# Weight halves of three projections added by transfers instead of VectorE, and four heads scaled during earlier scans

## The chip, the cores and the metric

The kernel runs on one core of one Trainium2 chip. The metric is the device time of one execution in microseconds (us), as the median of several runs. A profile of one execution shows what every engine did: TensorE (PE, its weight loads PEld), VectorE (DVE), ScalarE (ACT), GpSimd (POOL), and SyncE (SP), which here only issues transfers.

## The reference

Two requests, of 512 and 256 tokens, go through the same two layers of an encoder, 1024 wide. Each layer is `x += 1/2 FFN; x += mixer; x += 1/2 FFN` with an RMS norm ahead of each part. The mixer of the first layer is a gated linear recurrence run in both directions, with 8 heads of 128; that of the second layer is windowed attention. The change concerns the recurrent mixer alone:

```python
q, i, g, f_fw, f_bw = jnp.split(x @ w_in, 5, axis=-1)
...
o_fwd = gla_chunk_scan(q, k_f, i, logf_f)
o_bwd = rev(gla_chunk_scan(rev(q), rev(k_b), rev(i), rev(logf_b)))
o = (o_fwd + o_bwd).astype(F32)
o = o * lax.rsqrt(jnp.mean(o * o, axis=-1, keepdims=True) + NORM_EPS)
o = o * g_norm.astype(F32).reshape(H, V)
o = o.reshape(B, T, H * V).astype(x.dtype) * jax.nn.silu(g)
return o @ w_o
```

So the output of every head is divided by its own root mean square, gated with silu(g), and projected.

## The kernel before

All 768 tokens are treated together, as 6 blocks of 128 tokens or two halves of 384. Every operand of a large matrix product is split into a high part (a cast on ScalarE) and a low part (a subtraction on VectorE), and a product is made of three matmuls, high x high, high x low and low x high (`split`, `mm3`).

Large products are done by a fast scheme with seven products of half-sized blocks, p1 to p7, in place of eight. The weight matrix is cut into four blocks a11, a12, a21, a22, and the scheme needs sums of them. In the mixer three projections work so: **v** (the reference's `i`), **g** and the output projection **o**. `tok_steps` prepares their weights. It fetches the four blocks with transfers on SP's queue (each block as one tile `wr` of 128x1024 for the first half of its depth, kp = 0, and two tiles `tA` of 128x512 for the second, kp = 1), fetches a21 a second time into `s3`, and adds, with accumulating transfers on GpSimd's queue (`into`, line 147), a11 to that copy and a22 to a21. What it returns are 14 steps, one for each product and kp, in the order of the products: `TOK` for v and g (p1, p2, p7, p6, p5, p4, p3), `OUT` for o (p1, p2, p3, p7, p6, p4, p5). A step splits the block that its product needs into two tiles `w` (lines 323 and 324). There are 8 such tiles, so steps run as earlier products give theirs back.

Two more sums are needed. The "second" is a11 + a21, for p6; the "fourth" is a12 plus that, for p3. Before, both are additions on VectorE: in v and g ahead of the split of p6 and of p3 (line 260), in o both behind the split of p2 (line 272). They are held in program order. Every other instruction is ordered within its engine by a planner, which takes the program's order as a priority and has a model of durations; each engine's queue then runs strictly in the order that was planned.

`tok_quad` runs the seven products on TensorE (line 764). Several products share an accumulation bank: in o, p7 goes on in the bank of p3 after ScalarE has copied p3 out (line 1140). After p1 and p2 of o, `mixed` makes the sums of the activation blocks on VectorE (`mix`, lines 426 to 432) and splits them; line 1147 adds p2 to the residual.

Between v and g lie the eight scans, one for each head. A scan has seven levels: ScalarE copies the keys into a packed order (line 857), TensorE forms scores (line 827), VectorE merges them through masks (line 846) and multiplies queries (line 879), keys (line 883) and decays (line 885). After the levels come transposes, states and outputs (lines 900 to 938), and the sum of squares of the head's output goes into `hss` (line 939). `weave` puts pieces of other TensorE work between the levels: products for the gates and queries of the following heads (`stream`; lines 318 to 320, with sigmoids at line 803), and, from the end of the seventh scan on, the projection g (`gate`).

The norm of the heads is `rstds` (a square root on ScalarE, line 1030, which needs a table load, and a reciprocal, line 1031) and `scaled` (for each head six multiplications of 128x128 on ScalarE, line 1078). Before, the heads 0 to 6 get their `rstds` after the seventh scan, and each is scaled behind one level of the eighth scan; head 7 follows after it.

Of the kernel before, what the change touches and what calls it, by code (L numbers as in the profile page):

```python
# [25 lines left out]
HEADS = 8  # L26
# [18 lines left out]
TOK = ("p1", "p2", "p7", "p6", "p5", "p4", "p3")  # L45
TCHAIN = {"p2": "p1", "p4": "p5", "p3": "p7"}
OUT = ("p1", "p2", "p3", "p7", "p6", "p4", "p5")
# [5 lines left out]
class Trunk:  # L53
# [174 lines left out]
    def tok_steps(self, key, srcs, order):  # L228
        nc = self.nc
        flat = lambda t: t.rearrange("p a b -> p (a b)")  # L230

        def fetch(src):
            t = self.wp.tile([P, 1024], F32, tag="wr", name=self.name("wr"), bufs=RAWBUFS)
            nc.sync.dma_start(t.rearrange("p (a b) -> p a b", a=2), src[0])
            parts = [[t], [self.tmp(512), self.tmp(512)]]
            for a, t in enumerate(parts[1]):
                self.last_load = nc.sync.dma_start(t, src[1][:, a, :])
            return parts

        a11, a12, a21, a22 = (fetch(src) for src in srcs)  # L240
        more = self.big([P, 2, 512])
        s3 = [
            [self.wp.tile([P, 512], F32, tag="s3", name=self.name("s3"), bufs=2) for _ in range(2)],
            [more[:, a, :] for a in range(2)],
        ]
        for kp in range(2):
            for a, t in enumerate(s3[kp]):
                self.last_load = nc.sync.dma_start(t, srcs[2][kp][:, a, :])
                self.into(t, a11[0][0][:, a * 512 : (a + 1) * 512] if kp == 0 else a11[1][a])
            for t, u in zip(a21[kp], a22[kp]):  # L250
                self.into(t, u)
        own = {"p1": a11, "p2": a12, "p3": a12, "p4": a22, "p5": a21, "p6": a11, "p7": s3}
        second, fourth = (a11, a21), (a12, a11)
        sums = {"p6": (second,), "p3": (fourth,)} if order == TOK else {}
        behind = {"p2": (second, fourth)} if order == OUT else {}

        def step(name, kp):
            for total, part in sums.get(name, ()):
                for t, u in zip(total[kp], part[kp]):
                    self.tc.keep_in_program_order(nc.vector.tensor_add(t, t, u))  # L260
            hi, lo = self.wtile(), self.wtile()
            at = 0
            for src in own[name][kp]:
                n = src.shape[-1]
                h, l = (t[:, at : at + n] for t in (hi, lo))
                self.split(src, h, l)
                at += n
            view = lambda t: t.rearrange("p (a b) -> p a b", a=2)
            self.staged[(*key, name, kp)] = (view(hi), view(lo), 2)
            for total, part in behind.get(name, ()):  # L270
                for t, u in zip(total[kp], part[kp]):
                    self.tc.keep_in_program_order(nc.vector.tensor_add(t, t, u))

        return [(2, lambda name=name, kp=kp: step(name, kp)) for name in order for kp in range(2)]

    def stage_next(self):
# [698 lines left out]
    def hgrn(self, lb_row, gn_row, next_row):  # L975
        nc = self.nc
# [4 lines left out]
        heads = [{} for _ in range(HEADS)]  # L981
# [35 lines left out]
        scan = lambda hd: self.hgrn_scan(hd, vs)  # L1017

        def stream():
            for h in range(1, HEADS):  # L1020
                for c in (0, 3, 4):
                    if (h, c) not in LEAD:
                        yield from self.hgrn_chunk(h, heads[h], c, range(2))
                self.hgrn_gates(h, heads[h])
# [3 lines left out]
        def rstds(a, b):  # L1028
            r = rs[:, a:b, :]
            nc.scalar.activation(r, self.hss[:, a:b, :], AF.Sqrt, bias=self.eps, scale=1.0 / P)  # L1030
            nc.vector.reciprocal(r, r)
# [42 lines left out]
        def scaled(first, last):  # L1074
            for b in range(NBLK):
                for h in range(first, last):
                    u = vs[b][:, h * P : (h + 1) * P]
                    nc.scalar.activation(u, u, AF.Copy, scale=rs[:, h, b : b + 1])
# [21 lines left out]
        def gate():  # L1100
            need = {"p1": "t3", "p2": "t2", "p7": "t1", "p6": "t4"}
            for at in self.tok_quad(("g",), TOK, TCHAIN, self.ops, evac_g):
                if at[1:] == (HB - 1, 1) and at[0] in need:
                    self.reload_factor(need[at[0]])
                yield at

        feed = itertools.chain(stream(), gate())
        for h in range(HEADS - 1):
            self.weave(scan(heads[h]), feed, 16 if h == 0 else 18)
        rstds(0, HEADS - 1)  # L1110
        self.weave(scan(heads[-1]), feed, 20, also=lambda i: i < HEADS - 1 and scaled(i, i + 1))
        rstds(HEADS - 1, HEADS)
        scaled(HEADS - 1, HEADS)
        for i in range(HB):
# [441 lines left out]
```

## Time and profile before

| | |
|---|---|
| median of 3 runs | 2783.34 us (2783.18 to 2783.43) |
| the profiled execution: its own time | 2783.55 us |
| its span in the trace | 2781.6 us |
| TensorE busy in the span | 99% |
| mean granted TensorE clock | 0.998 |
| recurrent mixer | from about 503 to 1071 us of the span |
| v, scans, g, o on TensorE | from 542, 600, 878 and 967 us |

How to read it: a row of a timeline has start and length in us, the engine, the line of the kernel, the operation, what it writes and reads, shapes and the number of instructions merged into the row; square brackets hold the idle time of the engine before it and what ended that. "A <-B L5" means that A waited for what engine B did at line 5. Matmuls overlap, so TensorE can be busy all the time only as far as the rows show it.

### The profile page before, as it was taken

The numbers are of one execution on the slowest core, as the hardware profiler recorded it, in microseconds if no ns is written. First come the engines' busy times: TensorE is split into PE (matmuls) and PEld (weight loads), VectorE is DVE, ScalarE is ACT, GpSimd is POOL, SyncE is SP. The second block draws the span as 40 slices with busy tenths as digits, with TensorE's granted clock in tenths as the row PEclk, the third lists the DMA queues.
The fourth block names the chain that finished last, engine by engine and source line by source line (L and its number), as shares of the span: only waits on it lengthen the run. The fifth ranks groups of instructions, "written<-read, shape, count | busy, mean of one in ns | idle before, by whom it ended". The sixth has DMA issues, their size and how long they took to land.

```text
span 2781.6 us, 40766 instructions
## 1 busy us (share of the span) xinstructions
PE 2750.1 (99%) x15117; PEld 2555.3 (92%) x15117; DVE 2228.3 (80%) x3825; ACT 1387.6 (50%) x2586; POOL 393.9 (14%) x431
## 2 busy tenths in 40 slices
PE   8999999999999999999999999999999999999998
PEld 8999999989999879999999999999888889999998
DVE  8788788777887888788878887887848878788877
ACT  7344443634445765444445543444458855444443
POOL 2111121100000001211111121111102211211111
PEclk9999999999999999999999999999999999999999
DMA  6554554731121533655444355544422123655443
GB/s 173 128 126 117 126 141 123 244 107 39 39 67 50 173 92 81 147 133 129 117 113 119 81 144 134 124 122 114 129 73 76 45 63 75 146 133 129 117 115 107
DMA packets 337351, 313.41 MB, mean 113 GB/s; under 512 B 12584, under 2 KB 258816, under 8 KB 337152
## 3 DMA queue, kind: packets, MB, share of 16 engines
q1 hardware_dynamic: 296992, 221.81, 27.1%
q0 software_dynamic: 35856, 75.51, 15.0%
q10 hardware_dynamic: 4304, 13.49, 1.3%
q8 instruction: 119, 1.95, 0.3%
q14 instruction: 80, 0.66, 0.1%
HBM read 225.82 MB, written 15.73 MB: 87 GB/s over the span
## 4 chain that ended last, share of the span: by engine, by line
PE 95%; DVE 2%; ACT 2%; DMA 0%; issue 0%; DVEq 0%; ACTq 0%
PE ps L517 42%; PE ps L581 21%; PE ps L319 6%; PE ps L318 6%; PE ps L320 6%; PE ps L764 5%; PE ps L827 3%; PE ps L932 1%; PE ps L1418 1%; PE ps L908 1%; PE ps L389 1%; PE ps L1430 0%; PE ps L1380 0%; PE ps L1381 0%; PE ps L1431 0%; PE ps L1181 0%
## 5 line engine op out<-in xcount | busy, mean ns | idle before, releaser
L517 PE MATMUL ps<-big,w 128*128 128x384 f32 x6720 | 1169.3, 334 | 0.0
L517 PEld LDWEIGHTS ps<-big,w 128*128 128x128 f32 x6720 | 1165.9, 188 | 1.7 <-ACT tA L534 0.2
L208 ACT CAST w<-wr 128x512 fp32r<-128x512 f32 x600 | 416.0, 707 | 682.6 <-PE ps L517 274.2
L581 PE MATMUL ps<-w,big 128*128 128x512 f32 x2520 | 575.6, 389 | 0.0
L581 PEld LDWEIGHTS ps<-w,big 128*128 128x128 f32 x2520 | 472.6, 188 | 97.9 <-DVE x L603 0.3
L209 DVE TENSOR_TENSOR w<-wr,w 128x512 fp32r<-128x512 f32 (+1 forms) x520 | 430.3, 831 | 156.6 <-ACT w L208 140.1
L603 DVE SCALAR_TENSOR_TENSOR x<-ps,x 128x512 f32<-128x512 f32 x468 | 301.9, 683 | 10.1 <-PE ps L320 10.0
L147 POOL DMA_DIRECT2D s<-wr x126 | 110.9, 885 | 1353.5 <-DMA s<-in_ffn_w_dram 410.0
L318 PE MATMUL ps<-big,w 128*128 128x384 f32 x640 | 219.3, 345 | 2.0 <-ACT w L175 1.0
L319 PE MATMUL ps<-big,w 128*128 128x384 f32 x640 | 215.5, 337 | 0.9 <-DVE big L324 0.9
L320 PE MATMUL ps<-big,w 128*128 128x384 f32 x640 | 214.5, 335 | 0.0
L323 ACT CAST big<-tA 128x384 fp32r<-128x384 f32 x296 | 148.0, 513 | 114.3 <-DVE tA L549 36.4
L764 PE MATMUL ps<-w,big 128*128 128x512 f32 x756 | 179.7, 395 | 3.2 <-ACT big L1140 2.6
L764 PEld LDWEIGHTS ps<-w,big 128*128 128x128 f32 x756 | 141.4, 189 | 33.5 <-ACT big L1140 3.5
L324 DVE TENSOR_TENSOR big<-tA,big 128x384 fp32r<-128x384 f32 x296 | 166.2, 572 | 6.6 <-ACT big L323 4.5
L209 POOL TENSOR_TENSOR w<-wr,w 128x512 fp32r<-128x512 f32 x80 | 136.0, 1700 | 187.2 <-ACT w L208 182.8
L147 POOL DMA_DIRECT2D wr<-wr x103 | 90.8, 882 | 459.5 <-DMA wr<-in_ffn_w_dram 175.3
L318 PE MATMUL ps<-w,big 128*128 128x512 f32 x336 | 134.7, 401 | 0.3 <-DVE big L1441 0.2
L215 DVE TENSOR_TENSOR wr<-wr,wr 128x512 f32<-128x512 f32 (+1 forms) x120 | 122.9, 1024 | 14.2 <-issue 10.2
L320 PE MATMUL ps<-w,big 128*128 128x512 f32 x336 | 132.2, 393 | 0.5 <-DVE big L404 0.5
L319 PE MATMUL ps<-w,big 128*128 128x512 f32 x336 | 131.6, 392 | 0.0
L318 PEld LDWEIGHTS ps<-big,w 128*128 128x128 f32 x640 | 119.9, 188 | 3.2 <-ACT w L175 1.3
(219 smaller groups left out, 3471.2 us busy)
## 6 DMA issues: line engine op xcount, KB each, us to landing
wr<-in_ffn_w_dram SPq DMA_DIRECT2D x264, 512.0 KB, 4.0
s<-wr POOLq DMA_DIRECT2D x126, 256.0 KB, 4.9
s<-in_ffn_w_dram SPq DMA_DIRECT2D x120, 256.0 KB, 3.3
wr<-wr POOLq DMA_DIRECT2D x80, 256.0 KB, 3.8
wr<-in_hg_w_in_dram SPq DMA_DIRECT2D x32, 512.0 KB, 3.9
wr<-wr POOLq DMA_DIRECT2D x23, 512.0 KB, 4.6
spill<-x ACTq DMA_DIRECT2D x12, 512.0 KB, 3.9
kept<-big POOLq DMA_DIRECT2D x8, 768.0 KB, 5.4
```

Source lines behind the costliest of these rows:

```text
L147: self.nc.gpsimd.dma_start(out, src, accum_op=ALU.add)
L208: nc.scalar.copy(h, src)
L209: (eng or nc.vector).tensor_sub(l, src, h.bitcast(F32))
L318: nc.tensor.matmul(out, a[0], b[0], start=first, stop=False)
L319: nc.tensor.matmul(out, a[0], b[1], start=False, stop=False)
L320: nc.tensor.matmul(out, a[1], b[0], start=False, stop=last)
L323: self.nc.scalar.copy(hi, src)
L324: self.nc.vector.tensor_sub(lo, src, hi.bitcast(F32))
L517: self.nc.tensor.matmul(ps, a[x], b[y], start=first and k == 0 and i == 0, stop=k == 3 and i == 2, skip_group_check=True,)
L581: nc.tensor.matmul(ps, a[x], w[y], start=name == chain and kp == 0 and q == 0, stop=kp == 1 and q == 2, skip_group_check=True,)
L603: self.nc.vector.scalar_tensor_tensor(x, ps, c, x, ALU.mult, ALU.add)
L764: nc.tensor.matmul(ps, x[:, sl], y, start=fresh and k == 0 and q == 0, stop=k == 3 and q == 2, skip_group_check=True,)
```

## The change

In v and g the second and the fourth sum become accumulating transfers on GpSimd's queue: a21 is added to a11 once p1's part of a11 is split, and a11 to a12 once p2's part of a12 is split. In o the second sum becomes such a transfer behind the split of p1, and the fourth stays an addition on VectorE behind the split of p2. For o the blocks are fetched in the order a21, a22, a11, a12.

The heads 0 to 3 get their `rstds` right after the fourth scan. From the fifth scan on, one of them is scaled behind the second and one behind the fifth level of a scan, as long as any are left: two in the fifth scan and two in the sixth. Heads 4 to 6 get their `rstds` after the seventh scan as before and are scaled behind the second, fourth and sixth level of the eighth.

```diff
-        a11, a12, a21, a22 = (fetch(src) for src in srcs)
+        got = {i: fetch(srcs[i]) for i in ((0, 1, 2, 3) if order == TOK else (2, 3, 0, 1))}
+        a11, a12, a21, a22 = (got[i] for i in range(4))
...
-        second, fourth = (a11, a21), (a12, a11)
-        sums = {"p6": (second,), "p3": (fourth,)} if order == TOK else {}
-        behind = {"p2": (second, fourth)} if order == OUT else {}
+        behind = {"p1": (a11, a21), "p2": (a12, a11)}
+        add = self.into if order == TOK else lambda t, u: self.tc.keep_in_program_order(nc.vector.tensor_add(t, t, u))
 
         def step(name, kp):
-            for total, part in sums.get(name, ()):
-                for t, u in zip(total[kp], part[kp]):
-                    self.tc.keep_in_program_order(nc.vector.tensor_add(t, t, u))
             hi, lo = self.wtile(), self.wtile()
...
-            for total, part in behind.get(name, ()):
-                for t, u in zip(total[kp], part[kp]):
-                    self.tc.keep_in_program_order(nc.vector.tensor_add(t, t, u))
+            if name in behind:
+                for t, u in zip(*(parts[kp] for parts in behind[name])):
+                    (self.into if name == "p1" else add)(t, u)
...
         for h in range(HEADS - 1):
-            self.weave(scan(heads[h]), feed, 16 if h == 0 else 18)
-        rstds(0, HEADS - 1)
-        self.weave(scan(heads[-1]), feed, 20, also=lambda i: i < HEADS - 1 and scaled(i, i + 1))
+            early = (lambda i, h=h: i in (1, 4) and len(ready) and scaled(*ready.pop(0))) if h > 3 else None
+            self.weave(scan(heads[h]), feed, 16 if h == 0 else 18, also=early)
+            if h == 3:
+                rstds(0, 4)
+                ready = [(i, i + 1) for i in range(4)]
+        rstds(4, HEADS - 1)
+        self.weave(scan(heads[-1]), feed, 20, also=lambda i: i in (1, 3, 5) and scaled(4 + i // 2, 5 + i // 2))
```

## The prediction

> **What bounds the kernel now.** I read the page first, then the busy time in stretches of 20 us over the recurrent mixer (about 503 to 1071 us), then the timelines of the stretches in which TensorE is not full.
>
> ```profile
> PE 2750.1 (99%) x15117; PEld 2555.3 (92%) x15117; DVE 2228.3 (80%) x3825; ACT 1387.6 (50%) x2586; POOL 393.9 (14%) x431
> ```
>
> TensorE (PE) is busy for 99% of the 2781.6 us span. The change takes no matmul away, so it can gain only where TensorE stands idle or runs at a lower clock. Stretches of the mixer, as TensorE, its weight loads, VectorE (DVE), ScalarE (ACT), GpSimd (POOL), then clock and transfers:
>
> ```profile
> 580.00:600.00 20.00, 20.00 (x92) 16.61 (x91) 12.39 (x16) 5.85 (x7) 1.79 (x2) 1.00 0.64 187
> 800.00:820.00 20.00, 20.00 (x149) 20.00 (x148) 14.44 (x26) 9.85 (x21) 0.00 (x0) 1.00 0.18 54
> 900.00:920.00 20.00, 17.34 (x94) 14.20 (x93) 17.28 (x31) 18.57 (x48) 0.00 (x0) 1.00 0.50 186
> 980.00:1000.00 20.00, 16.76 (x69) 12.88 (x68) 19.94 (x26) 12.73 (x21) 0.00 (x0) 0.97 0.15 43
> 1000.00:1020.00 20.00, 20.00 (x85) 16.39 (x84) 13.23 (x19) 9.17 (x16) 0.00 (x0) 0.95 0.31 89
> ```
>
> The first row is the value projection (v), the second the turn from the fourth scan to the fifth: TensorE is full in both. The third is the eighth scan: 2.66 us idle, with ScalarE at 18.57 of 20. The fourth is the output projection (o): 3.24 us idle, with VectorE at 19.94 of 20, and clocks of 0.97 and 0.95 there and in the row after it, worth 0.03 x 20 + 0.05 x 20 = 1.6 us. So 2.66 + 3.24 + 1.6 = 7.5 us is what the change can reach; everything else it must not spoil.
>
> **The eighth scan: 24 of 42 scalings leave it.** TensorE, ScalarE and VectorE where the idle time lies:
>
> ```profile
> 907.94 1.58 PE L827 MATMUL ps<-big,big 128*128 128x128 f32 x12 [0.71 <-DVE big L879]
> 909.28 2.99 PE L764 MATMUL ps<-w,big 128*128 128x512 f32 x12
> 914.22 1.60 PE L827 MATMUL ps<-big,big 128*128 128x128 f32 x12 [1.95 <-ACT big L857]
> ```
> ```profile
> 909.45 1.04 ACT L323 CAST w<-wr 128x1024 fp32r<-128x1024 f32 x1
> 910.39 3.04 ACT L1078 ACTIVATE x<-x,hrs 128x128 f32<-128x128 f32 x10
> 913.33 0.83 ACT L857 COPY big<-big 128x768 f32<-128x768 f32 x1
> ```
> ```profile
> 912.20 1.02 DVE L883 TENSOR_TENSOR big<-big,big 128x384 f32<-128x384 f32 x2
> ```
>
> The two waits, 0.71 and 1.95 us, are the whole 2.66. The scores (L827) need ScalarE's copy of the keys (L857), which stands behind ten scalings (L1078). But L857 also reads what L883 wrote until 913.22, so VectorE is nearly as late, and there two additions for the g projection (L260) are queued in the same stretch. Their prices, and that of the scalings from 892 to 922 us:
>
> ```profile
> L1078 ACT ACTIVATE x<-x,hrs 128x128 f32<-128x128 f32 x42 | 13.1, 392 | 0.0
> ...
> L1030 ACT ACT_TABLE_LOAD x1 | 1.3, 1283 | 0.0
> ```
> ```profile
> L260 DVE TENSOR_TENSOR tA<-tA,tA x8: 682/684/690, 562.3 to 955.8; 128x512 f32<-128x512 f32 x8
> L260 DVE TENSOR_TENSOR wr<-wr,wr x4: 1216/1220/1220, 552.8 to 952.3; 128x1024 f32<-128x1024 f32 x4
> ```
>
> ScalarE loses 24 x 13.1 / 42 = 7.5 us of work in this scan. VectorE loses the addition before p6 of g, 1.22 + 2 x 0.68 = 2.6 us. Both things that L857 waits for come earlier. I return the 1.95 in full and half of the 0.71, since VectorE stays busy: 1.95 + 0.35 = **2.3 us gained**, between 0 (the chain through VectorE holds L827 as it is) and 2.66.
>
> **Scans five and six: the scalings arrive.** The code takes two heads in the fifth scan and two in the sixth; for the seventh none is left. ScalarE in the fifth:
>
> ```profile
> 808.04 0.91 ACT L857 COPY big<-big 128x768 f32<-128x768 f32 x1 [0.40 <-ACT x L938]
> 811.76 1.05 ACT L175 CAST w<-wr 128x1024 fp32r<-128x1024 f32 x1 [2.81 <-PE ps L319]
> 812.72 0.48 ACT L803 ACTIVATE big<-ps 128x384 f32<-128x384 f32 x1
> 814.98 0.84 ACT L857 COPY big<-big 128x768 f32<-128x768 f32 x1 [1.78 <-issue]
> ```
>
> A head is 6 x 13.1 / 42 = 1.87 us. Added once are a square root with its table load, and a table load back for the next sigmoid (L803): 1.28 + 0.3 + 1.28 = 2.9 us. So between the two L857 stand 2.9 + 1.87 = 4.8 us of new work against 2.81 + 1.78 = 4.6 us of idle time. The copy that ends at 815.82 is used by the scores at 817.53 in the chain that ended last:
>
> ```profile
> 817.53 1.34 PE ps L827 x12
> ```
>
> That leaves another 1.7 us. The other three heads have only 1.87 us each to hide. I cost it at **0**, hidden by ScalarE's waits; with that cover gone it is 2.9 + 4 x 1.87 = 10.4 us. The early square root waits for VectorE's sum of the fourth scan, and behind it on ScalarE stand the next L857 and the evacuations: that wait lies in the same slack.
>
> **Additions by transfer in v and g.** Twelve L260 become twelve transfers on GpSimd's queue. The transfer waits for the split of p1 (or p2) and for the one before it; behind it wait only GpSimd's own transfers and mask copy. What there is of time, by the last split of p2 and the first of p6 in v, and the prices of such transfers over the kernel (KB, us to landing; the last row takes in plain loads of tA too):
>
> ```profile
> 543.10 1.14 ACT L323 CAST w<-tA 128x512 fp32r<-128x512 f32 x2
> ...
> 557.37 1.05 ACT L323 CAST w<-wr 128x1024 fp32r<-128x1024 f32 x1 [0.55 <-PE ps L764]
> ```
> ```profile
> wr<-wr POOLq DMA_DIRECT2D x23, 512.0 KB, 4.6
> ...
> tA<-tA POOLq DMA_DIRECT2D x6, 256.0 KB, 6.7
> ```
> ```profile
> DMA to landing us min/median/max: 3.7/5.4/10.3
> ```
>
> p1 is split before p2, so the sum for p6 has over 14 us against 4.6 to 10.3. In g it is longer still: p6 is split at 909.45 (above), p1 during the sixth scan or before. The second sum is due only at p3. **0**, since TensorE has no idle time in v (first row of the stretches) and VectorE's relief there buys nothing.
>
> **The output projection.** TensorE waits three times; VectorE and ScalarE beside it:
>
> ```profile
> 988.17 6.19 PE L764 MATMUL ps<-w,big 128*128 128x512 f32 x26 [0.63 <-DVE w L324]
> 996.66 1.21 PE L764 MATMUL ps<-w,big 128*128 128x512 f32 x4 [2.30 <-ACT big L1140]
> 998.18 5.08 PE L764 MATMUL ps<-w,big 128*128 128x512 f32 x14 [0.31 <-ACT big L1140]
> ```
> ```profile
> 974.66 2.49 DVE L272 TENSOR_TENSOR tA<-tA,tA 128x512 f32<-128x512 f32 x4
> 977.07 0.95 DVE L426 TENSOR_TENSOR big<-big,big 128x768 f32<-128x768 f32 x1
> 979.87 0.69 DVE L1147 TENSOR_TENSOR x<-ps,x 128x512 f32<-128x512 f32 x1 [1.85 <-PE ps L764]
> 980.48 0.95 DVE L427 TENSOR_TENSOR big<-big,big 128x768 f32<-128x768 f32 x1
> ```
> ```profile
> L272 DVE TENSOR_TENSOR tA<-tA,tA x4: 684/685/685, 974.7 to 976.5; 128x512 f32<-128x512 f32 x4
> L272 DVE TENSOR_TENSOR wr<-wr,wr x2: 1218/1218/1219, 971.2 to 972.9; 128x1024 f32<-128x1024 f32 x2
> ```
>
> 0.63 + 2.30 + 0.31 = 3.24 us. p7 starts late because L1140, which frees its bank, and the split of its weights both come behind the mixing (L426 to L432), which fills VectorE. The change takes half of L272 off VectorE: 1.22 + 2 x 0.685 = 2.6 us. What that is worth hangs on one row: at 979.87 VectorE waits 1.85 us for TensorE (L1147), with L427 behind it. If the planner keeps that order, the 2.6 us only lengthen the wait: 0. If L427 and its like move ahead of L1147, the mixing ends 2.6 us earlier, the idle time falls to about 0.6 us, and the clock loss goes in part or whole: 2.6 to 4.2 us. I take **2.2 us**, about the middle. The row decides neither way, since how the order comes out isn't in it.
>
> The clock falls here after 3.24 us of idle time in three pieces, and not in the eighth scan after 2.66. The Trainium skill (TensorE: Matmul & The Clock Gate, What's actually happening) has the clock halved after an idle window of about 3.4 us. By that rule a wait cut to 0.6 us returns the whole 1.6, and the output projection alone would give 4.2 us; the trace, with a drop after shorter waits, does not quite fit the number.
>
> The transfers here: before, GpSimd adds a22 to a21 in this place.
>
> ```profile
> 963.85 1.79 POOL L147 DMA_DIRECT2D tA<-tA  x2 [0.51 <-DMA tA<-in_hg_w_o_dram]
> ```
>
> With a21 and a22 fetched first, that is done earlier, and the same sizes are issued for a11 + a21 once p1 is split, also near 964. At the median of 6.7 us the last, issued about 965, lands near 972, before the second addition on VectorE needs it (974.66 and after). So fetch order and new wait cost 0.
>
> **Sum.** The profiled run took 2783.55 us, 1.95 more than its span and 0.21 above the median of 2783.34. 2783.55 - 2.3 - 2.2 = 2779.05, or **2778.8 us** by the median. About 0.2%, 5.6 us, is what a measurement here can tell from no change, so this is within it.
>
> **Rivals.**
> - Both places in full: 2.66 + 3.24 + 1.6 = 7.5 us, 2775.8. For it: both have one crowded engine, and the change relieves it. Against: L883 and L1147.
> - The output projection keeps its order and gains nothing; only the scan does: 2781.0.
> - Slower: the new wait on VectorE decides. L272 waits for the two 256 KB transfers of a11; behind it on VectorE stand L426, the splits of p3 and p7 and all of the mixing, for which ScalarE and TensorE wait. It decides from a landing at 977.15 - 2 x 0.685 = 975.8. If the two follow one another at the longest time, they land at 965 + 2 x 10.3 = 985.6, and VectorE is 9.8 us late; the wait at L1147 takes up 1.85, the scan returns 2.3, and the longer idle time costs another 1.6 of clock: +7.2 us, 2790.5. Against it: transfers of one queue overlap, and the spill reloads that share the engines now were there already.
> - It does nothing: the planner puts other ScalarE work before L857, and VectorE's chain holds the scan: 2783.3.
>
> **How the numbers follow.** Forecast 0.44, with a range of its own from 2776.6 to 2781; both in full 0.18; scan alone 0.16; slower 0.16; nothing 0.06. Faster by over 0.2% (under 2777.8): all of the full case and 0.08 of the forecast's lower end, 0.26. Slower by over 0.2% (over 2788.9): most of its rival, 0.14. The rest, 0.60, is within. For 8 in 10 the range runs from 2775.0, past the full case, to 2787.0, which leaves out the longest transfers.
>
> **What would show it.** Right: between 890 and 945 us no wait of L827 over 0.5 us, with 18 scalings there and 24 between 806 and 890; TensorE still 20.00 of 20 at the turn from the fourth scan to the fifth; no L260; three L272 in place of six; in the output projection less idle time before p7 and clocks nearer 1.00. Wrong: a wait of L272 for a landing; L827 waiting in scans five or six behind L1078 or a table load; or the wait before p7 as long as now.

## The result and the profile after

The changed kernel takes **2776.06 us** (median of 9 runs, 2775.8 to 2777.32), against 2783.34 us before: 7.28 us less, a ratio of 0.9975 with a 95% interval of 0.9965 to 0.9985. That is inside the range given for 8 in 10 (2775.0 to 2787.0), but 0.5 us below the forecast's own (2776.6 to 2781): the forecast of 2778.8 was too small a gain. A gain of over 0.2% had been given 0.26, and a time within 0.2% of before 0.60, so the less likely of the two came. The time is nearest to the rival in which both places gain in full (2775.8), but by its mechanism it is not that rival, since 1.66 us of idle time stay in the output projection (below). The profiled execution took 2777.32 us, with a span of 2775.5, 6.1 less than before; it is the longest of its nine, so what follows explains 6.1 us of span, and the 1.2 us from there to the median difference stay open.

The lines of the kernel have moved: the former 1078 is 1075, 1030 is 1027, 857 is 854, 827 is 824, 803 is 800, 324 is 321, 764 is 761, the mixing 426 to 432 is 423 to 429, the addition of o (272) is 255; behind the loop over heads lines move up by one (1140 is 1141, 1147 is 1148). The stretches of the prediction, in the changed kernel (TensorE, weight loads, VectorE, ScalarE, GpSimd, clock, transfers):

```profile
580.00:600.00 20.00, 20.00 (x93) 16.65 (x92) 10.32 (x13) 5.95 (x7) 1.78 (x2) 1.00 0.60 144
800.00:820.00 20.00, 20.00 (x148) 20.00 (x147) 14.49 (x26) 9.85 (x21) 0.00 (x0) 1.00 0.17 54
900.00:920.00 20.00, 20.00 (x115) 17.42 (x113) 19.81 (x38) 14.38 (x28) 0.00 (x0) 1.00 0.66 240
980.00:1000.00 20.00, 18.34 (x80) 14.34 (x79) 19.22 (x26) 13.63 (x22) 0.00 (x0) 1.00 0.28 79
1000.00:1020.00 20.00, 20.00 (x90) 16.58 (x89) 13.28 (x20) 13.88 (x24) 0.00 (x0) 1.00 0.18 53
```

In the eighth scan TensorE's idle time is gone (2.66 to 0), and the crowded engine is now VectorE, at 19.81. In the output projection the idle time is 1.66 us instead of 3.24, and the clock stays at 1.00, which returns 1.6 us. 2.66 + 1.58 + 1.6 = 5.8 of the 6.1 us.

ScalarE where the scalings went (start, length, line, what, number):

```profile
765.76 1.28 ACT L1027 ACT_TABLE_LOAD   x1
767.06 0.32 ACT L1027 ACTIVATE hrs<-hss,eps 128x24 f32<-128x24 f32 x1
767.28 0.92 ACT L854 COPY big<-big 128x768 f32<-128x768 f32 x1
768.10 2.17 ACT L1075 ACTIVATE x<-x,hrs 128x128 f32<-128x128 f32 x7
770.16 0.47 ACT L800 ACTIVATE big<-ps 128x384 f32<-128x384 f32 x1
770.53 1.04 ACT L175 CAST w<-wr 128x1024 fp32r<-128x1024 f32 x1
771.47 1.87 ACT L1075 ACTIVATE x<-x,hrs 128x128 f32<-128x128 f32 x6
773.24 0.84 ACT L854 COPY big<-big 128x768 f32<-128x768 f32 x1
773.96 1.88 ACT L1075 ACTIVATE x<-x,hrs 128x128 f32<-128x128 f32 x6
775.85 1.28 ACT L800 ACT_TABLE_LOAD   x1
777.15 0.49 ACT L800 ACTIVATE big<-ps 128x384 f32<-128x384 f32 x1
777.53 0.83 ACT L854 COPY big<-big 128x768 f32<-128x768 f32 x1
778.26 1.57 ACT L1075 ACTIVATE x<-x,hrs 128x128 f32<-128x128 f32 x5
```

7 + 6 + 6 + 5 = 24: all four heads are scaled within 12 us of the fifth scan, none in the sixth. The planner took them into ScalarE's waits as soon as it found any, whatever level the code had put them behind. That stretch before and after:

```profile
760.00:780.00 20.00, 20.00 (x143) 20.00 (x142) 15.42 (x27) 9.38 (x20) 0.00 (x0) 1.00 0.09 27
```
```profile
760.00:780.00 20.00, 20.00 (x144) 20.00 (x143) 15.68 (x28) 18.78 (x46) 0.00 (x0) 1.00 0.09 27
```

ScalarE goes from 9.38 to 18.78 of 20 us, and TensorE stays full: the price is nothing, but almost nothing is left.

The output projection after, on TensorE and VectorE:

```profile
985.03 7.70 PE L761 MATMUL ps<-w,big 128*128 128x512 f32 x32 [1.35 <-DVE w L321]
993.04 10.29 PE L761 MATMUL ps<-w,big 128*128 128x512 f32 x44 [0.31 <-ACT big L1141]
```
```profile
970.43 1.29 DVE L255 TENSOR_TENSOR tA<-tA,tA 128x512 f32<-128x512 f32 x2
971.63 1.82 DVE L423 TENSOR_TENSOR big<-big,big 128x768 f32<-128x768 f32 x2
973.37 0.95 DVE L424 TENSOR_TENSOR big<-big,big 128x768 f32<-128x768 f32 x1
976.46 0.69 DVE L1148 TENSOR_TENSOR x<-ps,x 128x512 f32<-128x512 f32 x1 [2.14 <-PE ps L761]
```

VectorE still waits for TensorE before it adds p2 to the residual (2.14 us instead of 1.85), but three steps of the mixing now stand ahead of that wait where one did. The wait of 2.30 us before p7 is gone; one of 1.35 before p3's second half is larger than the 0.63 it replaces.

### The profile page after: what moved, and what is told of

It reads as the page before. It is cut to its first block, busy times and chain, and to the rows that moved or that the text cites. A ratio compares the mean times of both kernels' runs of the same rounds, so it can differ in the third digit from the quotient of the medians.

```text
span 2775.5 us, 40784 instructions
## 1 busy us (share of the span) xinstructions
PE 2748.4 (99%) x15117; PEld 2554.6 (92%) x15117; DVE 2223.5 (80%) x3811; ACT 1390.9 (50%) x2589; POOL 409.9 (15%) x446
## 3 DMA queue, kind: packets, MB, share of 16 engines
q8 instruction: 119, 1.95, 0.3%
## 4 chain that ended last, share of the span: by engine, by line
PE 95%; DVE 2%; ACT 2%; DMA 0%; issue 0%; DVEq 0%; ACTq 0%; SPq 0%
PE ps L514 42%; PE ps L578 21%; PE ps L316 6%; PE ps L315 6%; PE ps L317 6%; PE ps L761 5%; PE ps L824 3%; PE ps L929 1%; PE ps L1419 1%; PE ps L905 1%; PE ps L386 1%; PE ps L1431 0%; PE ps L1381 0%; PE ps L1382 0%; PE ps L1432 0%; PE ps L1182 0%
## 5 line engine op out<-in xcount | busy, mean ns | idle before, releaser
L209 DVE TENSOR_TENSOR w<-wr,w 128x512 fp32r<-128x512 f32 (+1 forms) x520 | 437.7, 846 | 148.5 <-ACT w L208 131.0
```

The source lines that it names most:

```text
L209: (eng or nc.vector).tensor_sub(l, src, h.bitcast(F32))
```

## The experiments

All medians are set against the kernel before on the same chip; the runs below were on three chips, and its medians there were 2783.04 to 2783.18. Beside a difference stands the ratio with its 95% interval, which reaches some 2.5 us either way. My theory at the outset was the prediction's: the scalings decide in the eighth scan, the sum taken off VectorE decides in the output projection, and the transfers of v and g buy nothing. The rivals: VectorE's additions for g were the limit of the scan, or the output projection gained only by what came to it from earlier.

**The scalings alone** (`e_scale`): the kernel before with the change of the loop over heads.

```diff
...
+            if h == 3:
+                rstds(0, 4)
+                ready = [(i, i + 1) for i in range(4)]
+        rstds(4, HEADS - 1)
+        self.weave(scan(heads[-1]), feed, 20, also=lambda i: i in (1, 3, 5) and scaled(4 + i // 2, 5 + i // 2))
```

> The kernel before with the scalings moved alone. Theory (ScalarE's ten scalings ahead of the key copy were what TensorE waited for in the eighth scan): the 2.66 us of idle time between 900 and 920 us go almost wholly, 2.3 to 3.2 us faster than before, about 2780.5; the output projection keeps its 3.24 us of idle time and its lowered clock. Rival (VectorE's two additions for g in that scan were the limit): at most 0.7 us faster, with waits of over 1 us left before the scores.

2780.85 us, 2.2 less (ratio 0.9992, 0.9983 to 1.0001; the interval just takes in no change, so the gain rests on the idle time below as much as on the median). **The sums of v and g by transfers alone** (`e_vg`):

```diff
-        sums = {"p6": (second,), "p3": (fourth,)} if order == TOK else {}
+        behind = {"p1": (a11, a21), "p2": (a12, a11)}
+        add = self.into if order == TOK else lambda t, u: self.tc.keep_in_program_order(nc.vector.tensor_add(t, t, u))
...
+            if order == OUT:
+                if name == "p2":
...
+            elif name in behind:
+                for t, u in zip(*(parts[kp] for parts in behind[name])):
+                    (self.into if name == "p1" else add)(t, u)
```

> The kernel before with the sums of v and g by transfers alone; scalings and output projection as before. Theory: within 0.5 us of before, since ScalarE's queue in the eighth scan is as long as it was; the idle time of 2.66 us there stays above 2. Rival (VectorE): 2 to 3 us faster, and the idle time in the eighth scan goes here.

2782.68 us, 0.4 less (0.9999, 0.9990 to 1.0007), no change that can be told. The eighth scan in the first and in the second of these:

```profile
900.00:920.00 20.00, 19.41 (x109) 16.40 (x108) 19.67 (x35) 13.44 (x26) 0.00 (x0) 1.00 0.46 179
```
```profile
900.00:920.00 20.00, 18.14 (x104) 15.39 (x103) 17.23 (x32) 19.42 (x47) 3.14 (x4) 1.00 0.81 271
```

Of 2.66 us idle the scalings alone leave 0.59, the transfers alone 1.86 (over 2 was expected); together nothing is left. So ScalarE was the larger part, and the rival holds for the rest: the last 0.59 us go only when VectorE is relieved too.

**The output projection alone** (`e_o`): second sum by transfer and the new fetch order, all else as before.

```diff
+        got = {i: fetch(srcs[i]) for i in ((0, 1, 2, 3) if order == TOK else (2, 3, 0, 1))}
...
-        behind = {"p2": (second, fourth)} if order == OUT else {}
+        behind = {"p1": (second,), "p2": (fourth,)} if order == OUT else {}
...
+                    if name == "p1":
+                        self.into(t, u)
+                    else:
```

> The kernel before with the output projection's second sum by transfer and its new fetch order alone. Theory (2.6 us less on VectorE let the mixing start earlier): idle time there falls from 3.24 to about 1.7 us and the clock stays at 1.00, 3 to 4 us faster than before, about 2780; the eighth scan is as before. Rival (the output projection gained in the changed kernel only because TensorE came to it less delayed or because g's additions had left VectorE): under 1 us faster.

2787.24 us, **4.2 slower** (1.0014, 1.0005 to 1.0023). Neither theory had that. **The scalings and the output projection** (`e_scale_o`), the changed kernel with v's and g's sums on VectorE:

> The changed kernel with the sums of v and g back on VectorE. Theory (those transfers buy nothing): 2776 to 2776.6, as the changed kernel; the scan and the output projection each keep their gain, and the two add. Rival (VectorE's additions for g take part in the limit of the eighth scan): 0.7 to 2.5 us slower than the changed kernel, with waits of the scores coming back between 900 and 920 us.

2784.31 us, 1.3 more than before (1.0002, 0.9994 to 1.0011) where the changed kernel has 7.3 less (6.4 when it was run again, below): 7.7 to 8.6 apart, far beyond the rival's 2.5. The output projection in `e_o` and in `e_scale_o`:

```profile
980.00:1000.00 20.00, 14.79 (x48) 11.09 (x47) 18.12 (x24) 10.39 (x16) 0.00 (x0) 0.74 0.21 71
```
```profile
980.00:1000.00 20.00, 15.83 (x59) 12.08 (x58) 19.49 (x25) 13.44 (x21) 0.00 (x0) 0.83 0.15 44
```

TensorE is idle for 5.21 and 4.17 us, against 3.24 before, and clocks of 0.74 and 0.83 cost another 5.2 and 3.4 us, against 1.6 before. In both, the mechanism of the prediction's slower rival is there. The second additions on VectorE (line 276 in these two) in `e_scale_o`:

```profile
973.31 1.23 DVE L276 TENSOR_TENSOR wr<-wr,wr 128x1024 f32<-128x1024 f32 x1 [3.09 <-DMA wr<-wr]
...
975.87 0.69 DVE L276 TENSOR_TENSOR tA<-tA,tA 128x512 f32<-128x512 f32 x1 [0.73 <-DMA tA<-tA]
978.36 0.69 DVE L276 TENSOR_TENSOR tA<-tA,tA 128x512 f32<-128x512 f32 x1 [1.79 <-DMA tA<-tA]
```

VectorE waits 3.09 + 0.73 + 1.79 = 5.6 us for the transfers of a11 (7.2 us in `e_o`), with all the mixing behind it. Why they are late is on GpSimd's queue, and on SP's, which loads the third `wr` tile, a11, at 951.54:

```profile
951.54 0.38 SPq L234 DMA_DIRECT2D wr<-in_hg_w_o_dram  x1
```
```profile
955.85 1.75 POOL L147 DMA_DIRECT2D s<-wr  x2 [12.61 <-DMA wr<-in_hg_w_o_dram]
957.02 1.50 POOL L147 DMA_DIRECT2D big<-tA  x1
963.12 0.87 POOL L147 DMA_DIRECT2D big<-tA  x1 [4.60 <-issue]
964.80 0.86 POOL L147 DMA_DIRECT2D wr<-wr  x1 [0.81 <-DMA big<-tA]
```

In the changed kernel the third tile is loaded at 932.81, and the transfer into a11 is issued at 957.98:

```profile
932.81 0.38 SPq L234 DMA_DIRECT2D wr<-in_hg_w_o_dram  x1
```
```profile
957.98 0.86 POOL L147 DMA_DIRECT2D wr<-wr  x1 [10.51 <-DVE w L321]
```

The transfer thus goes out 6.8 us later in `e_scale_o`. Half of that is p1's split, which ends at 961.0 instead of 957.6; the other half is the copies for `s3` that stand ahead of it. It also takes longer to land, 8.4 us instead of 5.2, while the transfers' share is 1.01 instead of 0.71 from 960 to 980 us.

The new theory: g's a11 was held until VectorE had added it into a12, just ahead of p3; in `e_scale_o` that addition ends at 951.51 and the load starts at 951.54. With g's sums by transfer behind p1 and p2, g's a11 comes free after p6's split, at 907.99. The projection's first load takes its buffer at 908.01, every later load moves up by one buffer, and the third, a11, starts some 19 us earlier, in time for its copies of `s3` to be out of GpSimd's queue when a11 itself is due. Four runs (`e_vg_o`, `e_scale_vg`, `e_order`, `e_v_dve`) test what follows from that. None changes the buffers alone, for example by adding more of them, so that the buffer, and not the work that leaves VectorE, decides rests on the rows above: the load starts as the addition ends, and VectorE stands waiting for a landing.

**All but the scalings** (`e_vg_o`), the loop over heads as before:

> The changed kernel with the scalings back as before. The two runs with the output projection's new sum and g's sums on VectorE were slow in the output projection: VectorE's second addition waited there for a11's transfer, which came late because a11 was loaded only at 953 us. New theory: g's sums by transfer free g's a11 earlier, so that the output projection's a11 finds a buffer earlier; the output projection is then as in the changed kernel (idle about 1.7 us, clock 1.00) while the eighth scan keeps about 1.9 us of idle time: 2778 to 2779.5, 4 to 5 us faster than before. Rival (the scalings decide in the output projection too, by bringing the work there in another order): the output projection is slow here too, 2783 or more.

2779.03 us, 4.15 less (0.9986, 0.9977 to 0.9995), as the new theory has it, and so is the output projection:

```profile
980.00:1000.00 20.00, 18.34 (x79) 14.33 (x79) 19.94 (x27) 13.52 (x22) 0.00 (x0) 1.00 0.25 72
```

**All but the output projection** (`e_scale_vg`):

> The changed kernel with the output projection's sums and fetch order as before. New theory: the eighth scan without idle time, 2.7 to 3.2 us gained there, and nothing gained in the output projection (idle 3.2 us and a lowered clock): 2780 to 2781. Rival (g's transfers alone help the output projection, by their buffers, whatever is done there): 2777 to 2778.

2779.06 us, 4.1 less (0.9987, 0.9978 to 0.9996), 0.9 below the expected 2780 to 2781, which stays unexplained. The eighth scan is full and the output projection keeps its wait before p7 and its lowered clock, as expected, so the sum by transfer is needed there; the rival falls.

```profile
992.73 5.60 PE L765 MATMUL ps<-w,big 128*128 128x512 f32 x17 [2.29 <-ACT big L1145]
```
```profile
980.00:1000.00 20.00, 17.09 (x68) 13.28 (x68) 19.37 (x27) 12.06 (x19) 0.00 (x0) 0.91 0.27 78
```

**The old fetch order** (`e_order`), all else changed:

```diff
-        got = {i: fetch(srcs[i]) for i in ((0, 1, 2, 3) if order == TOK else (2, 3, 0, 1))}
+        got = {i: fetch(srcs[i]) for i in (0, 1, 2, 3)}
```

> The changed kernel with the output projection's blocks fetched in the old order a11, a12, a21, a22. New theory (the transfer that adds a21 to a11 needs a21 + a22 first, and with this order those load last): VectorE's second addition waits for it by 3 us or more, idle time and a lowered clock come back in the output projection, 2779 to 2784. Rival (the order of the fetches is no matter as long as g's buffers come free early): 2776 to 2777.

2776.85 us (0.9977, 0.9968 to 0.9986), as expected of the changed kernel: the rival holds, and the order of the fetches is no part of the gain once g's sums go by transfer. The old order with g's sums on VectorE was not tried. The a21 + a22 transfers go out at 952.52 to 955.18 in this run, still ahead of a11's:

```profile
952.52 0.86 POOL L147 DMA_DIRECT2D wr<-wr  x1 [33.41 <-DVE big L1057]
953.95 0.88 POOL L147 DMA_DIRECT2D tA<-tA  x1 [0.56 <-DVE x L1069]
955.18 0.87 POOL L147 DMA_DIRECT2D tA<-tA  x1 [0.35 <-issue]
957.93 0.86 POOL L147 DMA_DIRECT2D wr<-wr  x1 [1.87 <-DVE big L1059]
```

**v's sums back on VectorE** (`e_v_dve`), which leaves g's share:

```diff
+        sums = {"p6": (a11, a21), "p3": (a12, a11)} if key == ("v",) else {}
+        if sums:
+            behind = {}
...
```

> The changed kernel with v's sums back on VectorE; g, o and the scalings as changed. Theory (v has idle room on VectorE, and v's buffers are not what anyone waits for): as the changed kernel within 0.5 us. Rival (v's blocks coming free earlier help the loads of the first scans): 0.5 to 2 us slower.

2776.38 us (0.9974, 0.9964 to 0.9984), beside 2776.70 for the changed kernel on that chip: v's six transfers buy nothing, g's do it all.

**The 24 scalings in one block** (`e_bunch`), behind the second level of the fifth scan:

```diff
-            early = (lambda i, h=h: i in (1, 4) and len(ready) and scaled(*ready.pop(0))) if h > 3 else None
+            early = (lambda i, h=h: i == 1 and len(ready) and (scaled(0, 4), ready.clear())) if h > 3 else None
```

> The changed kernel with all 24 early scalings behind the second level of the fifth scan, in one block, instead of four blocks over two scans. Theory (a block of 1.87 us is hidden in ScalarE's wait for the scores and the copy's lead of 1.5 us): a block of 7.5 us with the two table loads is longer than the 4.6 us of wait and the lead together, so TensorE waits 2 to 4 us before the third level's scores, 2778 to 2780. Rival (the planner spreads the 24 over the next levels, or ScalarE has room anyway): under 1 us slower than the changed kernel.

2782.44 us (0.9998, 0.9989 to 1.0007), 5.7 more than the changed kernel beside it and 2.4 above the expected range; nearly the whole gain is lost.

```profile
771.00 5.08 ACT L1075 ACTIVATE x<-x,hrs 128x128 f32<-128x128 f32 x17
776.10 1.28 ACT L800 ACT_TABLE_LOAD   x1
777.40 0.49 ACT L800 ACTIVATE big<-ps 128x384 f32<-128x384 f32 x1
777.78 0.82 ACT L854 COPY big<-big 128x768 f32<-128x768 f32 x1
```
```profile
760.00:780.00 20.00, 16.52 (x116) 16.20 (x115) 11.96 (x21) 17.57 (x44) 0.00 (x0) 0.93 0.09 27
780.00:800.00 20.00, 20.00 (x125) 20.00 (x125) 15.27 (x28) 6.88 (x9) 1.75 (x2) 0.90 0.25 53
```

17 scalings and the table load stand ahead of the key copy, TensorE is idle 3.48 us, and the clock takes another 0.07 x 20 + 0.10 x 20 = 3.4. The idle time is as expected, but the expectation had no term for the clock. The same 24 instructions cost nothing when the planner can lay a key copy between them, and 5.7 us when it can't: within one emitted block it did not put the later copy first.

**The changed kernel again** (`after_again`), as the measure for its neighbours:

> The changed kernel once more, as the measure for the three others: 2776 to 2777.

2776.70 us (0.9976, 0.9967 to 0.9985), as expected: 6.4 less than the kernel before on that chip, where the first measurement had 7.3.

**The fourth sum of o by transfer as well** (`e_o_fourth`, and again as `fourth_again` beside the changed kernel):

```diff
-        add = self.into if order == TOK else lambda t, u: self.tc.keep_in_program_order(nc.vector.tensor_add(t, t, u))
+        add = self.into
```

> The changed kernel with the output projection's fourth sum by transfer as well. Theory: VectorE loses another 2.6 us where it is the limit, but the split of p3 on ScalarE waits for two transfers in a row, which land some 10 us after p1's split: if they land by 978 us, the idle time of 1.7 us before p3 and p7 shrinks and the kernel is 0.5 to 1.5 us faster than the changed one; if later, ScalarE's queue stands behind that wait and it is 1 to 4 us slower. Rival (VectorE isn't the limit any more in the output projection): no change, 2776 to 2777.

> The changed kernel with the output projection's fourth sum by transfer, once more, beside the changed kernel on the same chip. Theory (VectorE was still the limit there): 1.3 to 2 us faster than the changed kernel. Rival (the difference of the first run was one between chips): within 0.5 us of it.

2774.39 us (0.9969, 0.9957 to 0.9980), and again 2775.04 (0.9971, 0.9960 to 0.9982): 1.7 us less than the changed kernel on the same chip, whose runs (2776.24 to 2777.37) do not overlap with these (2774.30 to 2775.91). The output projection in `fourth_again`:

```profile
980.00:1000.00 20.00, 19.86 (x88) 16.08 (x87) 17.94 (x26) 11.60 (x19) 0.00 (x0) 1.00 0.28 79
```

Idle 0.14 instead of 1.66 us: VectorE was still the limit there, and ScalarE's cast for p3, which now waits for two transfers in a row, is not held up (it starts at 973.78 in the first of the two runs, 974.24 in the changed kernel). This version beats both kernels, by some 8 and 1.7 us.

| against before, us | o's sums as before | o changed |
|---|---|---|
| scalings and v, g as before | 0 | +4.2 |
| scalings moved | -2.2 | +1.3 |
| v, g by transfer | -0.4 | -4.15 |
| both | -4.1 | -7.3 and -6.4 |

Read from the left column to the right: the change of o costs 3.5 to 4.2 us without g's transfers and gains 2.3 to 3.75 with them. Each cell is uncertain by some 2.5 us, and three of them (-2.2, -0.4 and +1.3) can't be told from no change by themselves; +4.2, -4.1 and -4.15 can, and the idle time and VectorE's waits in the traces go the same way.

## Why the prediction was right and where it was wrong

- **What bounds the kernel**: right. What could be reached was 7.5 us in three rows, and 5.8 us came from these. That the median's 7.28 lies so near 7.5 is in part luck: the rest of it was not found in these rows.
- **The eighth scan**, 2.3 us taken, 2.66 measured; moving the scalings is worth 2.2 to 3.7 us by the table. The half of 0.71 us held back for VectorE is real: 0.59 us stay idle without g's transfers.
- **Scans five and six**: the price of 0 is right (TensorE 20.00 before and after), by rows of the wrong place. The rows at 808 to 817, which I took for the turn from the fourth scan to the fifth, are in the sixth; the fifth begins near 765. Its idle pattern is the same, so the sum survived. That the 24 would lie over two scans, between 806 and 890, was wrong: all are in the fifth.
- **The additions by transfer in v and g, priced at 0**: the step that failed. Alone they give 0.4 us, but I looked only at when their results are due, not at when the buffers that they read come free. g's are the condition for the whole gain in the output projection: without them its change costs 3.5 to 4.2 us instead of gaining 2.3 to 3.75. So the total came out in range by luck in this term: the price of 0 for the new wait in the output projection held only through an effect of these transfers that I had not seen.
- **The output projection**, 2.2 us taken as the middle of 0 and 4.2; 1.58 of idle time and 1.6 of clock came back, 3.2 us. The size was off since L1148 kept its place and two more mixing steps moved ahead of it, something between the two orders that I had left open. That the fetch order serves the sum fell: with the old order the time is the same.
- **The slower rival**, put at 0.16, is what this change does without g's transfers, with waits of 5.6 and 7.2 us on VectorE. My reason against it (transfers of one queue overlap) was not why it stayed away: the queue ahead was emptied earlier.

## What to carry to other kernels

When a sum moves to another engine, follow its operands' buffers as well as its result: here six transfers that saved no time by themselves let a load start 19 us earlier, and decided whether another part of the change gained 2.3 to 3.75 us or lost about 4. Test parts of a change alone and together, since the sign of one can hang on another. Work that is to fill an engine's waits should be emitted in pieces that a planner can lay other work between: the same 24 instructions cost TensorE nothing in four pieces and the kernel 5.7 us in one.

## What the runs showed of the hardware that I had not expected

The clock can fall after shorter waits than I had thought. In the output projection a wait of 2.29 us, after one of 0.63 some eight us earlier, took the 20 us around it to 0.91 and cost 0.09 x 20 = 1.8 us (`e_scale` and `e_scale_vg`). The Trainium skill (TensorE: Matmul & The Clock Gate, What's actually happening) gives an idle window of about 3.4 us; by these rows less than that is enough here.

The length of a wait does not decide alone. A single wait of TensorE of 1.95 us (eighth scan before) left the clock at 1.00, as did one of 1.86 in the run without the scalings. But the attention of the second layer has a wait of 1.89 us near 2173 us in both profiles of the changed kernel, and the 10 us from 2170 have a clock of 0.83 in one (`after`) and 1.00 in the other (`after_again`). So the cut from 2.30 to 1.35 us in the output projection gained twice, by the wait and by the clock; that any wait cut to under 2 us keeps the clock is not shown, and what decides is open.
